# Block products for gate and up (seven of 256 columns for eight), and the down projection as a last stage

## The chip, the cores and the metric

The kernel runs on 1 core of one Trainium2 chip. The metric is the device time of one execution in microseconds (us), from the profiler's clock of that core. The core has five engines with queues of their own: TensorE (PE; its weight loads are shown apart as PEld), VectorE (DVE), ScalarE (ACT), GpSimd (POOL) and SyncE (SP), which issues all the large DMAs here in the order of its own queue.

## The reference

One encoder layer on 512 tokens, d = 2048, in float32. Attention (a differential and a latent half, not touched here) gives `mix`; then an output projection and a gated feed-forward network of 5632 features. The six vectors of `mod` scale, shift and gate.

```python
mod = c_act @ w_ada[l] + b_ada[l]
sh1, sc1, gt1, sh2, sc2, gt2 = [m[:, None, :] for m in jnp.split(mod, 6, axis=-1)]
...
mix = jnp.concatenate([a_out, b_out], axis=-1) @ w_out[l]
x = x + gt1 * mix
h2 = rms_norm(x, g_norm2[l]) * (1 + sc2) + sh2
ffn = (jax.nn.silu(h2 @ w_gate[l]) * (h2 @ w_up[l])) @ w_down[l]
x = x + gt2 * ffn
```

## The kernel before

**Arithmetic.** Every float32 product is made of three matmuls (`mm3`, lines 231 to 233): both operands are split into a high part (a cast, `hi`, line 79 on ACT) and a low part (the difference, `lo`, line 87, in turn on DVE and on POOL), and high x high, high x low and low x high are summed in PSUM.

**Weights.** The class `Weights` follows a plan, a list of chunks of 128 x 1024 float32 (512 KB) in the order of use. A chunk is loaded by SP (line 62) into one of three `raw` buffers and split into one of two `hi` and two `lo` buffers; `get` returns a chunk, splits the next and loads the one after it.

**Stages.** The input projection and the attention come first (not touched). The output projection ends at about 972 us of the profile: four column blocks b, each a `project` into four PSUM banks (`ps_o`), with the side work of `second_modulation` between its steps: loads of w_ada (line 289) and multiply-adds into `adaacc` on DVE (line 296), which give the scale and shift of the second norm; `MOD_PACE` says how many such steps go to one step of the projection. `residual` (lines 1048, 1049) adds the block to `x1`, which stays in SBUF, and `transposes` brings it into `x1T`. After `second_norm` the activations h2 lie in SBUF as high and low parts, features on the partitions and 512 tokens in the columns.

**Feed-forward.** `gate_up(j)` makes one pair: 256 gate and 256 up features, 16 steps over d, two blocks of 128 features each, all 512 tokens wide: 192 matmuls of 512 columns. The result act = silu(g) * u is split into `ah` and `al` (line 1160). The 22 pairs go in parts of `PARTS` = 4, 4, 4, 4, 3, 3; after each part `down` multiplies its acts by w_down, again in four column blocks, and adds the product times the gate vector `gt2` to x1 in SBUF; in the last part each tile of x1 is stored. The vector `gt2` itself (`gate2`) is computed as side work of the first `gate_up` calls, with loads of w_ada of its own. The order on PE is that of the program; a scheduler orders the other engines.

## Time and profile before

| | us |
|---|---|
| median of 3 runs (lowest, highest) | 2420.62 (2419.66, 2422.67) |
| the profiled execution | 2424.76 |
| its span in the trace | 2422.9 |
| PE busy in it | 2289.0 |
| DVE busy | 1284.9 |
| ACT busy | 789.7 |
| POOL busy | 786.2 |

The span goes from the first to the last instruction in the trace; the time of the execution has 1.9 us around it. The mean granted clock of TensorE is 0.981 of full speed (1 is 2.4 GHz, 0.5 is 1.2 GHz). The feed-forward part takes the span from about 973 us to its end.

### The profile page before, as it was taken

Reading aid. Unit: us, or ns where it says so; the run is one execution under the profiler, and the core shown is the slowest. Engines: PE = TensorE matmul, PEld = TensorE weight load, DVE = VectorE, ACT = ScalarE, POOL = GpSimd, SP = SyncE. Lnnn points to the kernel's source line nnn. Section 1 sums busy time; section 2 is a strip of 40 time slices with the busy share of each in tenths; the row PEclk is TensorE's granted clock in tenths of the full one; section 3 lists DMA queues with packets and bytes.
Section 4 is the critical chain, followed back from the end, with each engine's and each line's share of the span. In section 5 each row is a group of like instructions: output and inputs, shape, how many; then the busy total and the mean of one; then the engine's idle time right before and its main releaser. Section 6 shows DMA issues by size and latency. Waiting matters only on the chain.

```text
span 2422.9 us, 28819 instructions
## 1 busy us (share of the span) xinstructions
PE 2289.0 (94%) x10998; PEld 1949.5 (80%) x10998; DVE 1284.9 (53%) x1883; ACT 789.7 (33%) x1359; POOL 786.2 (32%) x671
## 2 busy tenths in 40 slices
PE   3878998998999988999999999999999999999999
PEld 2777998997777767788888888888888888888887
DVE  6998876877988479754242114322241224314324
ACT  4433454557555323422212222122212221222121
POOL 1668744436544513121212222221212122222211
PEclk9989999999999989999999999999999999999999
DMA  8765443532433577444232333333233333333333
GB/s 278 211 198 161 137 146 110 178 90 92 151 124 113 182 239 243 152 160 144 89 103 94 97 96 96 96 96 100 93 103 93 99 96 96 96 96 96 95 100 127
DMA packets 262573, 313.11 MB, mean 129 GB/s; under 512 B 13949, under 2 KB 186470, under 8 KB 262306
## 3 DMA queue, kind: packets, MB, share of 16 engines
q1 hardware_dynamic: 261944, 310.91, 40.8%
q8 instruction: 86, 1.41, 0.2%
q10 hardware_dynamic: 490, 0.36, 0.1%
q14 instruction: 53, 0.43, 0.1%
HBM read 306.99 MB, written 4.24 MB: 128 GB/s over the span
## 4 chain that ended last, share of the span: by engine, by line
PE 62%; DVE 3%; DMA 3%; issue 1%; POOL 0%; ACT 0%; SPq 0%; DVEq 0%; POOLq 0%
PE ps_g L231 7%; PE ps_g L233 7%; PE ps_g L232 7%; PE ps_d L232 7%; PE ps_d L231 7%; PE ps_d L233 7%; PE ps_u L233 7%; PE ps_u L232 7%; PE ps_u L231 7%; DMA araw<-in_w_ada_dram 2%; DVE adaacc L296 2%; DVE lo L87 0%; PE ps_o L233 0%; DVE tm L1048 0%; DVE x L1049 0%
## 5 line engine op out<-in xcount | busy, mean ns | idle before, releaser
L87 POOL TENSOR_TENSOR lo<-raw,hi 128x1024 fp32r<-128x1024 f32 (+1 forms) x188 | 439.9, 2340 | 1318.0 <-ACT hi L79 1313.3
L79 ACT CAST hi<-raw 128x1024 fp32r<-128x1024 f32 (+2 forms) x388 | 390.0, 1005 | 1137.9 <-PE ps_d L232 327.9
L87 DVE TENSOR_TENSOR lo<-raw,hi 128x1024 fp32r<-128x1024 f32 (+2 forms) x200 | 234.1, 1171 | 855.1 <-ACT hi L79 854.0
L296 DVE SCALAR_TENSOR_TENSOR adaacc<-araw,c_col,adaacc 128x256 f32<-128x256 f32 (+1 forms) x334 | 296.9, 895 | 34.1 <-DMA araw<-in_w_ada_dram 21.2
L231 PE MATMUL ps_g<-h2h,hi 128*128 128x512 f32 x704 | 274.8, 390 | 1.6 <-ACT h2h L1113 1.6
L233 PE MATMUL ps_g<-h2l,hi 128*128 128x512 f32 x704 | 274.7, 390 | 0.0
L232 PE MATMUL ps_g<-h2h,lo 128*128 128x512 f32 x704 | 274.7, 390 | 0.0
L233 PE MATMUL ps_u<-h2l,hi 128*128 128x512 f32 x704 | 273.9, 389 | 0.0
L231 PE MATMUL ps_u<-h2h,hi 128*128 128x512 f32 x704 | 273.9, 389 | 0.0
L232 PE MATMUL ps_u<-h2h,lo 128*128 128x512 f32 x704 | 273.9, 389 | 0.0
L231 PE MATMUL ps_in<-hi,hh 128*128 128x384 f32 (+2 forms) x704 | 242.6, 345 | 26.5 <-DVE raw_s L480 7.0
L233 PE MATMUL ps_in<-lo,hh 128*128 128x384 f32 (+2 forms) x704 | 235.5, 335 | 8.5 <-POOL lo L87 8.5
L232 PE MATMUL ps_in<-hi,hl 128*128 128x384 f32 (+2 forms) x704 | 234.9, 334 | 1.0 <-POOL hl L370 0.9
L232 PE MATMUL ps_d<-hi,al 128*128 128x512 f32 x512 | 199.5, 390 | 0.0
L231 PE MATMUL ps_d<-hi,ah 128*128 128x512 f32 x512 | 199.4, 389 | 0.0
L233 PE MATMUL ps_d<-lo,ah 128*128 128x512 f32 x512 | 199.2, 389 | 0.0
L231 PEld LDWEIGHTS ps_in<-hi,hh 128*128 128x128 f32 x704 | 138.8, 197 | 33.8 <-issue 9.5
L231 PEld LDWEIGHTS ps_g<-h2h,hi 128*128 128x128 f32 x704 | 132.7, 188 | 29.5 <-ACT h2h L1113 1.9
L233 PEld LDWEIGHTS ps_g<-h2l,hi 128*128 128x128 f32 x704 | 132.5, 188 | 28.3 <-DVE h2l L1114 0.7
L232 PEld LDWEIGHTS ps_g<-h2h,lo 128*128 128x128 f32 x704 | 132.6, 188 | 27.6
L233 PEld LDWEIGHTS ps_u<-h2l,hi 128*128 128x128 f32 x704 | 132.2, 188 | 27.4
L232 PEld LDWEIGHTS ps_u<-h2h,lo 128*128 128x128 f32 x704 | 132.1, 188 | 27.5
(267 smaller groups left out, 3852.9 us busy)
## 6 DMA issues: line engine op xcount, KB each, us to landing
araw<-in_w_ada_dram SPq DMA_DIRECT2D x128, 512.0 KB
raw<-in_w_gate_dram SPq DMA_DIRECT2D x88, 512.0 KB
raw<-in_w_up_dram SPq DMA_DIRECT2D x88, 512.0 KB
raw<-in_w_down_dram SPq DMA_DIRECT2D x88, 512.0 KB
ada<-in_w_ada_dram SPq DMA_DIRECT2D x128, 256.0 KB
raw<-in_w_in_dram SPq DMA_DIRECT2D x128, 192.0 KB
raw<-in_w_out_dram SPq DMA_DIRECT2D x32, 512.0 KB
xs<-in_x_dram SPq DMA_DIRECT2D x16, 256.0 KB
```

The costliest lines, as they stand in the source:

```text
L79: nc.scalar.copy(out=hi[:, :n], in_=raw[:, :n])
L87: e.tensor_tensor(out=lo[:, :n], in0=raw[:, :n], in1=hi[:, :n].bitcast(F32), op=ALU.subtract)
L231: pe.matmul(o, ah, bh, start=start, stop=False)
L232: pe.matmul(o, al, bh, start=False, stop=False)
L233: pe.matmul(o, ah, bl, start=False, stop=stop)
L296: dve.scalar_tensor_tensor(out=acc[:, :width], in0=raw[:, i, :width], scalar=c_col[:, q:q + 1], in1=acc[:, :width], op0=ALU.mult, op1=ALU.add)
```

## The change

Two pairs stay as they were (`STRAIGHT`). For the other 20, gate and up are made as separate **units** of 256 features. A unit's product is cut in two along features, along d and along tokens, and the eight block products are made from seven (the scheme of Strassen in Winograd's form): seven products of a sum of weight blocks (B11, B21, B22 and T1 to T4; 1024 x 128) with a sum of activation blocks (1024 x 256 tokens), 24 matmuls of 256 columns each, the high and low parts as before. The sums of activations (`comb`, seven of them, split) are built once, during the straight pairs (`combine`, run by `between`). The sums of weights are built for each unit on DVE; all splits of a unit's low parts are on DVE too (`prepare`), and the products are put together in a tile `cu` by ACT copies and DVE adds from PSUM (`unit`). Weights come in halves of 1 MB (`load_half`, three buffers `wr`), `hi` and `lo` have three buffers, and `AHEAD` = 2 products are prepared ahead. act goes to DRAM (`actd`), 0.5 MB a pair.

The down projection is one last stage in parts of 2, 4, 4, 4, 4, 4 pairs; `load_acts` reads act back and splits it. Sums over parts are kept in 16 SBUF tiles; x1 is stored to DRAM (`x1d`) in the output projection and read again in the last part but one. `gate2` is side work of parts 1 to 3 of the down stage. In the output projection the loads of w_ada are of 256 KB in place of 512, into 24 slots that x1, x1T and the accumulators share. What runs before the output projection keeps its order on each engine.

```diff
-PARTS = (4, 4, 4, 4, 3, 3)
+PARTS = (2, 4, 4, 4, 4, 4)
+STRAIGHT = 2
+X_SLOTS = 24
+W_BUFS = 3
+AHEAD = 2
+
+PRODUCTS = (("B11", 0, "X"), ("B21", 2, "Z"), ("T2", 5, "X"), ("T1", 4, "W"), ("T3", 1, "X"), ("T4", 3, "Y"),
+            ("B22", 6, "W"))
...
-    def pair(j):
+    for j in range(STRAIGHT):
         for k4 in range(4):
             for n in ("gate", "up"):
                 plan.append(((n, j, k4), [4, 256], rows(a["w_" + n][0], k4 * 512, 4, j * 256, 256), "alt"))
...
+    return plan
+
+
+def down_plan(a):
+    plan, j = [], 0
+    for n in PARTS:
         for b in range(4):
             for q in range(n):
-                plan.append((("down", b, j + q), [2, 512], rows(a["w_down"][0], (j + q) * 256, 2, b * 512, 512),
-                             "alt"))
+                src = a["w_down"][0][(j + q) * 256:(j + q + 1) * 256, b * 512:(b + 1) * 512]
+                plan.append((("down", b, j + q), [2, 512], src.rearrange("(k p) n -> p k n", p=P), "alt"))
         j += n
...
-    mod2 = second_modulation(raws2, accs2, MOD_EARLY, KC, 2)
+    def accs2(dt=F32):
+        return xtile("adaacc", dt)
+
+    mod2 = second_modulation(xtile, accs2, MOD_EARLY, KC, 1)
...
+            sp.dma_start(out=x1d[t * P:(t + 1) * P, b * 512:(b + 1) * 512], in_=x1[t][b])
...
+    def combine(p):
+        a11, a21 = [x1T[p][:, i * 256:(i + 1) * 256] for i in range(2)]
+        a12, a22 = [x1T[p + 8][:, i * 256:(i + 1) * 256] for i in range(2)]
+        r = [xtile("sr") for _ in range(2)]
+        s1, s2, s4 = r[0][:, :256], r[0][:, 256:], r[1][:, :256]
+        dve.scalar_tensor_tensor(out=s1, in0=a21, scalar=shs[:, p:p + 1], in1=a22, op0=ALU.add, op1=ALU.add)
+        dve.scalar_tensor_tensor(out=s2, in0=s1, scalar=SH2[:, p:p + 1], in1=a11, op0=ALU.subtract, op1=ALU.subtract)
+        dve.scalar_tensor_tensor(out=s4, in0=a12, scalar=SH2[:, p + 8:p + 9], in1=s2, op0=ALU.add, op1=ALU.subtract)
+        dve.tensor_tensor(out=s3[:, p], in0=a11, in1=a21, op=ALU.subtract)
+        for i, src in ((4, half_rows(r[0])), (6, s4.unsqueeze(1))):
+            n = src.shape[1]
+            act.copy(out=comb[p][:, i:i + n, 0, :], in_=src)
+            dve.tensor_tensor(out=comb[p][:, i:i + n, 1, :], in0=src, in1=f(comb[p][:, i:i + n, 0, :]),
+                              op=ALU.subtract)
...
+    def load_half(u, kh):
+        if u >= N_UNITS:
+            return
+        j, n = divmod(u, 2)
+        j += STRAIGHT
+        src = a["w_gate" if n == 0 else "w_up"][0][kh * 1024:(kh + 1) * 1024, j * 256:(j + 1) * 256]
+        t = fw[0][1].tile([P, 8, 256], F32, tag="wr", bufs=3, name="wr")
+        sp.dma_start(out=t, in_=src.rearrange("(k p) n -> p k n", p=P))
+        for n in range(2):
+            units.setdefault(u, {})[f"B{kh + 1}{n + 1}"] = t[:, :, tsl(n)]
...
+    def prepare(q):
+
+        if q >= LAST_Q:
+            Wd.split(q - LAST_Q)
+            return
+        u, i = divmod(q, 7)
+        w = units[u]
+        if i == 0:
+            w["T1"], w["T2"] = [wp.tile([P, 1024], F32, tag="lo", bufs=2, name="wt").rearrange(
+                "p (k n) -> p k n", k=8) for _ in range(2)]
+            w["T3"], w["T4"] = w["B12"], w["T2"]
+        out, x, y = {0: ("T1", "B12", "B11"), 1: ("T2", "B22", "T1"), 2: ("T3", "B22", "B12"),
+                     3: ("T4", "B21", "T2")}.get(i, (None,) * 3)
+        src = w[PRODUCTS[i][0]]
+        hi, lo = [fw[0][1].tile([P, 8, P], F32R, tag=n, bufs=W_BUFS, name=n) for n in ("wh", "wl")]
+        act.copy(out=hi, in_=src)
+        if i < 2:
+            minus(w[out], w[x], w[y])
+        minus(lo, src, f(hi))
+        if i in (2, 3):
+            minus(w[out], w[x], w[y])
+        split[q] = hi, lo
+
+    def multiply(q, ps):
+        u, i = divmod(q, 7)
+        _, ci, bk = PRODUCTS[i]
+        wh, wl = split.pop(q)
+        first = bk not in ps
+        if first:
+            ps[bk] = bank(tags[u % 2], "ps_" + bk)[:, :256]
+        for k in range(8):
+            c = comb[k][:, ci]
+            pe.matmul(ps[bk], wh[:, k], c[:, 0], start=first and k == 0, stop=False, skip_group_check=True)
+            pe.matmul(ps[bk], wh[:, k], c[:, 1], start=False, stop=False, skip_group_check=True)
+            pe.matmul(ps[bk], wl[:, k], c[:, 0], start=False, stop=k == 7, skip_group_check=True)
+        return ps[bk]
+
+    def unit(u):
+
+        ps = {}
+        cu = wp.tile([P, 1024], F32, tag="hi", bufs=2, name="cu").rearrange("p (c s) -> p c s", c=4)
+
+        def plus(i, j, b):
+            dve.tensor_tensor(out=cu[:, i], in0=cu[:, j], in1=b, op=ALU.add)
+
+        for i in range(7):
+            q = 7 * u + i
+            if i == 0:
+                load_half(u + 1, 0)
+            prepare(q + AHEAD)
+            b = multiply(q, ps)
+            if i == 0:
+                act.copy(out=cu[:, 0], in_=b)
+            elif i == 1:
+                plus(0, 0, b)
+            elif i == 2:
+                act.copy(out=cu[:, 2], in_=b)
+            elif i == 4:
+                act.copy(out=cu[:, 1], in_=b)
+                plus(3, 1, ps["W"])
+                load_half(u + 1, 1)
+            elif i == 5:
+                plus(1, 1, b)
+            elif i == 6:
+                plus(2, 2, b)
+            if u == N_UNITS - 1 and i in LATE:
+                LATE[i]()
+        return cu
...
+    def load_acts(i):
+        j0 = sum(PARTS[:i])
         r = []
...
+        for kt in range(2 * j0, 2 * (j0 + PARTS[i])):
+            if i == 0:
+                both = wp.tile([P, 1024], F32R, tag=("raw", "lo")[kt % 2], bufs=(3, 2)[kt % 2], name="act0")
+                ah, al = both[:, :512], both[:, 512:]
+                if kt % 4 == 0:
+                    avs = fw[0][1].tile([P, 8, 256], F32, tag="wr", bufs=3, name="av0").rearrange(
+                        "p (k a) b -> p k (a b)", k=4)
+                av = avs[:, kt % 4]
             else:
-                ah, al = slot("ah"), slot("al")
-            act.copy(out=ah, in_=sg)
-            dve.tensor_tensor(out=al, in0=sg, in1=f(ah), op=ALU.subtract)
+                ah, al = [fd[1].tile([P, S], F32R, tag="ax", bufs=32, name="ax") for _ in range(2)]
+                av = fd[1].tile([P, S], F32, tag="x1r", bufs=4, name="av")
+            sp.dma_start(out=av, in_=actd[kt])
+            act.copy(out=ah, in_=av)
+            minus(al, av, f(ah))
             r.append((ah, al))
...
+    def between():
+        for p in range(8):
+            if p == 0:
+                shift_sums()
+            combine(p)
+            if p in (1, 3, 4, 5, 6):
+                yield
+        close_pool(fp)
+        fw.append(open_pool("fw"))
+        load_half(0, 0)
+        load_half(0, 1)
+        yield
+        prepare(0)
+        yield
+        for q in range(1, AHEAD):
+            prepare(q)
...
+    for u in range(N_UNITS):
+        res = unit(u)
+        if u % 2 == 0:
+            g = res
+            act.activation(g, g, AF.Silu)
+        else:
+            ao = wp.tile([P, 1024], F32, tag="raw", bufs=3, name="ao").rearrange("p (c s) -> p c s", c=4)
+            dve.tensor_tensor(out=ao, in0=g, in1=res, op=ALU.mult)
+            j = u // 2 + STRAIGHT
+            sp.dma_start(out=actd[2 * j:2 * j + 2].rearrange("f p s -> p f s"),
+                         in_=ao.rearrange("p (f c) s -> p f (c s)", f=2))
+    turn[0] = 1 if tags[(N_UNITS - 1) % 2] == "tmp" else 0
+    close_pool(hp)
...
+    for i, n in enumerate(PARTS):
         for b in range(4):
             tag = next_tag()
+            spare[0] = "tmp" if tag == "acc" else "acc"
             pss = [bank(tag, "ps_d") for _ in range(NT)]
-            for _ in project(pss, acts, 512, [("down", b, j0 + q) for q in range(len(acts) // 2)]):
+            cs = slice(b * 512, (b + 1) * 512)
+            if b == 1 and 0 < i and i + 1 < n_parts:
+                load_acts(i + 1)
+            if i == n_parts - 2:
+                xr = []
+                for t in range(NT):
+                    xr.append(fd[1].tile([P, S], F32, tag="x1r", bufs=4, name="x1r"))
+                    sp.dma_start(out=xr[t], in_=x1d[t * P:(t + 1) * P, cs])
+            for _ in project(pss, acts[i], 512, [("down", b, j + q) for q in range(n)]):
+                if 0 < i < n_parts - 2:
+                    next(side, None)
+            for t in range(NT):
+                s = sums[t][b]
+                if i == 0:
+                    act.copy(out=s, in_=pss[t])
+                elif i < n_parts - 1:
+                    dve.tensor_tensor(out=s, in0=s, in1=pss[t], op=ALU.add)
+                    if i == n_parts - 2:
+                        dve.tensor_tensor(out=s, in0=s, in1=gt2[:, cs], op=ALU.mult)
+                        dve.tensor_tensor(out=s, in0=s, in1=xr[t], op=ALU.add)
+                else:
+                    tm = fd[1].tile([P, S], F32, tag="x1r", bufs=4, name="tm")
+                    dve.tensor_tensor(out=tm, in0=pss[t], in1=gt2[:, cs], op=ALU.mult)
+                    dve.tensor_tensor(out=s, in0=s, in1=tm, op=ALU.add)
+                    sp.dma_start(out=out[0, t * P:(t + 1) * P, cs], in_=s)
+        if i == n_parts - 3:
+            for _ in side:
                 pass
-            for t in range(NT):
-                residual(pss, b, t, gt2)
-                if last:
-                    sp.dma_start(out=out[0, t * P:(t + 1) * P, b * 512:(b + 1) * 512], in_=x1[t][b])
```

Three places where the order of instructions moves. **DVE, between two gate/up results.** Before, one pair: `lo` is the low part of a chunk, `sg` the Silu'd gate (times up from `ps_u`), `ax` its split; in brackets is what a row waits for (DMAHW a load, and engines by name).

```order
L87 TENSOR_TENSOR lo<-raw,hi 128x1024 [waits DMAHW0_49,Activation_49]
L1154 TENSOR_TENSOR sg<-sg,ps_u 128x512 [waits PE_49]
L1154 TENSOR_TENSOR sg<-sg,ps_u 128x512 [waits PE_49,Activation_49]
L1160 TENSOR_TENSOR ax<-sg,ax 128x512 [waits Activation_49] x2
L87 TENSOR_TENSOR lo<-raw,hi 128x1024 [waits DMAHW2_49,PE_49,Activation_49]
L87 TENSOR_TENSOR lo<-raw,hi 128x1024 [waits DMAHW4_49,PE_49,Activation_49]
```

After, one unit in the middle of the blocks (`wr` is a raw weight half or a sum written over it, `wt` a sum of weight blocks, `wl` a low part, `cu` the unit's result, `ps_Z`, `ps_W` and `ps_Y` products):

```order
L1205 TENSOR_TENSOR wt<-wr 128x1024 [waits DMAHW4_49,DVE_49]
L1250 TENSOR_TENSOR cu<-cu,ps_Z 128x256 [waits PE_49,Activation_49]
L1205 TENSOR_TENSOR wl<-wr,wh 128x1024 [waits Activation_49]
L1205 TENSOR_TENSOR wl<-wt,wh 128x1024 [waits PE_49,Activation_49]
L1205 TENSOR_TENSOR wl<-wr,wh 128x1024 [waits PE_49,Activation_49]
L1205 TENSOR_TENSOR wt<-wr,wt 128x1024 [waits DMAHW6_49,DVE_49]
L1205 TENSOR_TENSOR wr<-wr 128x8x128
L1250 TENSOR_TENSOR cu<-cu,ps_W 128x256 [waits Activation_49]
L1205 TENSOR_TENSOR wl<-wr,wh 128x1024 [waits PE_49]
L1250 TENSOR_TENSOR cu<-cu,ps_Y 128x256 [waits DVE_49,PE_49]
L1205 TENSOR_TENSOR wl<-wr,wh 128x1024 [waits Activation_49]
L1250 TENSOR_TENSOR cu<-cu,ps_W 128x256 [waits PE_49]
```

The row `wt<-wr,wt` with a DMA among its waits is the first that reads the second half of the next unit's weights; three rows of the present unit's and the next unit's work stand behind it and ahead of the add of `ps_Y`.

**SP, the end of the output projection and the first gate and up loads.** Before:

```order
L62 DMA raw<-in_w_out_dram 128x2x512
L289 DMA araw<-in_w_ada_dram 128x2x512 x2
L62 DMA raw<-in_w_out_dram 128x2x512
L289 DMA araw<-in_w_ada_dram 128x2x512 x2
L62 DMA raw<-in_w_gate_dram 128x4x256
L289 DMA araw<-in_w_ada_dram 128x2x512 x2
L62 DMA raw<-in_w_up_dram 128x4x256
L289 DMA araw<-in_w_ada_dram 128x2x512 x4
L62 DMA raw<-in_w_gate_dram 128x4x256
```

After (`x_` with a number is a slot of x1 or of a w_ada load):

```order
L301 DMA x_9961<-in_w_ada_dram 128x512
L1104 DMA x1d<-x_9134 128x512
L301 DMA x_9964<-in_w_ada_dram 128x512
L1104 DMA x1d<-x_9138 128x512
L301 DMA x_9979<-in_w_ada_dram 128x512
L1104 DMA x1d<-x_9142 128x512
L1104 DMA x1d<-x_9146 128x512
L74 DMA raw<-in_w_gate_dram 128x4x256
L74 DMA raw<-in_w_up_dram 128x4x256
L74 DMA raw<-in_w_gate_dram 128x4x256
L74 DMA raw<-in_w_up_dram 128x4x256
L1104 DMA x1d<-x_9135 128x512
```

The w_ada loads that stood between the first gate and up chunks are gone from there, and stores of x1 stand ahead of and behind them.

**SP, where gate 2's w_ada loads stand.** Before, between the weights of the first pairs:

```order
L62 DMA raw<-in_w_gate_dram 128x4x256
L62 DMA raw<-in_w_up_dram 128x4x256
L289 DMA araw<-in_w_ada_dram 128x2x512
L62 DMA raw<-in_w_gate_dram 128x4x256
L289 DMA araw<-in_w_ada_dram 128x2x512 x2
L62 DMA raw<-in_w_up_dram 128x4x256
L289 DMA araw<-in_w_ada_dram 128x2x512 x3
```

After, between the weights of the down stage, at the densest place:

```order
L74 DMA raw<-in_w_down_dram 128x2x512
L301 DMA araw<-in_w_ada_dram 128x2x512 x2
L74 DMA raw<-in_w_down_dram 128x2x512
L301 DMA araw<-in_w_ada_dram 128x2x512 x3
L74 DMA raw<-in_w_down_dram 128x2x512
L301 DMA araw<-in_w_ada_dram 128x2x512 x2
L74 DMA raw<-in_w_down_dram 128x2x512
L297 DMA adaacc<-in_b_ada_dram 1x512
```

They moved from the gate and up chunks to the down chunks, with up to three of them between two chunks.

## Rows read from the trace of the kernel before

**Rows 1.** The page, part 1: busy us, share of the span, instructions.

```profile
PE 2289.0 (94%) x10998; PEld 1949.5 (80%) x10998; DVE 1284.9 (53%) x1883; ACT 789.7 (33%) x1359; POOL 786.2 (32%) x671
```

**Rows 2.** The page, part 4: shares of the chain that ended last.

```profile
PE 62%; DVE 3%; DMA 3%; issue 1%; POOL 0%; ACT 0%; SPq 0%; DVEq 0%; POOLq 0%
```

**Rows 3.** Windows (us): length, busy us (count) by engine, clock, DMA share, GB/s.

```profile
815.00:850.00 35.00, 33.86 (x148) 27.34 (x147) 16.20 (x15) 8.70 (x13) 30.64 (x19) 1.00 0.84 277
850.00:890.00 40.00, 30.47 (x138) 24.86 (x139) 31.50 (x34) 8.89 (x12) 9.30 (x4) 0.94 0.72 238
890.00:930.00 40.00, 40.00 (x169) 33.37 (x169) 31.65 (x43) 10.11 (x17) 5.94 (x3) 0.85 0.77 261
...
950.00:975.00 25.00, 15.89 (x61) 11.67 (x60) 21.39 (x32) 9.70 (x19) 8.21 (x10) 0.70 0.62 205
...
1000.00:1200.00 200.00, 200.00 (x883) 165.28 (x882) 95.15 (x87) 51.51 (x60) 46.25 (x21) 1.00 0.45 145
...
1500.00:2000.00 500.00, 500.00 (x2201) 412.96 (x2200) 140.10 (x133) 113.92 (x124) 109.97 (x46) 1.00 0.31 96
```

**Rows 4.** Timeline of PE in the input projection: start, us, instruction.

```profile
453.89 0.28 PE L232 MATMUL ps_in<-hi,hl 128*128 128x256 f32 x1
...
456.89 0.28 PE L233 MATMUL ps_in<-lo,hh 128*128 128x256 f32 x1
...
476.30 0.33 PE L231 MATMUL ps_in<-hi,hh 128*128 128x256 f32 x1
476.47 0.28 PE L232 MATMUL ps_in<-hi,hl 128*128 128x256 f32 x1
...
480.54 0.28 PE L233 MATMUL ps_in<-lo,hh 128*128 128x256 f32 x1
```

**Rows 5.** The page, part 5, a group of weight loads: busy us, mean ns.

```profile
L231 PEld LDWEIGHTS ps_g<-h2h,hi 128*128 128x128 f32 x704 | 132.7, 188 | 29.5 <-ACT h2h L1113 1.9
```

**Rows 6.** Groups by line and form on DVE, ACT, POOL: busy us, mean ns, idle before.

```profile
L87 DVE TENSOR_TENSOR lo<-raw,hi 128x1024 fp32r<-128x1024 f32 x157 | 192.8, 1228 | 845.0 <-ACT hi L79 844.7 <-DMA raw<-in_w_gate_dram 0.3
L296 DVE SCALAR_TENSOR_TENSOR adaacc<-araw,c_col,adaacc 128x512 f32<-128x512 f32 x154 | 164.0, 1065 | 22.8 <-DMA araw<-in_w_ada_dram 13.8 <-DMA adaacc<-in_b_ada_dram 5.7
...
L1048 DVE TENSOR_TENSOR tm<-ps_d,gt 128x512 f32<-128x512 f32 x96 | 65.7, 685 | 28.4 <-PE ps_d L233 27.8
...
L785 DVE COPY kn<-ps_in 128x256 f32<-128x256 f32 x16 | 6.6, 411 | 0.2 <-issue 0.2
...
L79 ACT CAST hi<-raw 128x1024 fp32r<-128x1024 f32 x308 | 324.1, 1052 | 1084.6 <-PE ps_d L232 327.9 <-PE ps_u L233 279.7 <-PE ps_g L233 207.7
...
L1153 ACT ACTIVATE sg<-ps_g 128x512 f32<-128x512 f32 x44 | 26.2, 595 | 79.3 <-PE ps_g L233 79.3
...
L819 ACT COPY vr<-ps_in 128x256 f32<-128x256 f32 x16 | 6.0, 376 | 0.0
...
L87 POOL TENSOR_TENSOR lo<-raw,hi 128x1024 fp32r<-128x1024 f32 x151 | 367.6, 2435 | 1275.4 <-ACT hi L79 1275.4
```

**Rows 7.** Timeline of DVE and POOL in a down block.

```profile
1216.76 0.69 DVE L1049 TENSOR_TENSOR x<-x,tm 128x512 f32<-128x512 f32 x1
...
1218.08 2.76 DVE L1049 TENSOR_TENSOR x<-x,tm 128x512 f32<-128x512 f32 x1
...
1217.90 2.40 POOL L87 TENSOR_TENSOR lo<-raw,hi 128x1024 fp32r<-128x1024 f32 x1 [8.20 <-ACT hi L79]
```

**Rows 8.** The chain that ended last, 930 to 1010 us: start, us, what.

```profile
945.63 5.63 DMA araw<-in_w_ada_dram
...
953.38 4.30 DMA raw<-in_w_gate_dram
...
958.93 3.49 DMA raw<-in_w_up_dram
```

**Rows 9.** PE's waits from 800 us on: us in total, times, longest.

```profile
PE ps_o L233 <- DVE lo L87: 8.3, 3, 6.6
PE ps_xT L1055 <- DVE x L1049: 7.0, 4, 3.2
```

More of the change, by code (lines that the diff above doesn't have):

```diff
@@ L1099, in hybrid_layer, with h2, half_rows @@
     transposes(3, spare[0])
[L1100 removed]
+    rB = bank(tag, "ps_r")
     for t in range(NT):
[L1102 to L1104 removed]
+        pe.matmul(rB[:, tsl(t)], rstd2[:, t:t + 1].broadcast_to([P, P]), ident, start=True, stop=True)
+    close_pool(fo)
+    close_pool(big_pool)
+    hp, sx = open_pool("hp", "right"), open_pool("sx", "right")
+    comb = [hp[1].tile([P, 7, 2, 256], F32R, tag="comb", bufs=8, name="comb") for _ in range(8)]
+    s3 = sx[1].tile([P, 8, 256], F32, name="s3")
+    def h2(kc, part):
+        i = kc // 8 * 2
+        return comb[kc % 8][:, i:i + 2, part, :]
+    def half_rows(ap):
+        return ap.rearrange("p (a b) -> p a b", a=2)
     def second_norm(k0):
@@ L1162, in gate_up @@
-        return r
-    def down(j0, acts, last):
+                next(between, None)
+        sg = wp.tile([P, 1024], F32, tag="raw", bufs=3, name="sg").rearrange("p (m s) -> p m s", m=2)
+        for m in range(2):
+            act.activation(sg[:, m], pg[m], AF.Silu)
+            dve.tensor_tensor(out=sg[:, m], in0=sg[:, m], in1=pu[m], op=ALU.mult)
+        sp.dma_start(out=actd[2 * j:2 * j + 2].rearrange("f p s -> p f s"), in_=sg)
+    N_UNITS = 2 * (DFF // 256 - STRAIGHT)
+    LAST_Q = 7 * N_UNITS
@@ new lines, in hybrid_layer @@
+    units, split = {}, {}
+    fw = []
+    def load_half(u, kh):
[8 more added lines that the diff above has]
+            units.setdefault(u, {})[f"B{kh + 1}{n + 1}"] = t[:, :, tsl(n)]
@@ new lines, in hybrid_layer @@
+    second_norm(0)
+    def between():
[14 more added lines that the diff above has]
+            prepare(q)
+        yield
+    gate_up(0, iter(()))
+    for j in range(1, STRAIGHT):
+        mid = between() if j == STRAIGHT - 1 else iter(())
+        gate_up(j, mid)
@@ new lines, in hybrid_layer @@
+    for _ in mid:
+        pass
+    tags = ("acc", "tmp") if turn[0] else ("tmp", "acc")
+    for p in range(8):
+        act.copy(out=comb[p][:, 1, 0, :], in_=s3[:, p])
+        minus(comb[p][:, 1, 1, :], s3[:, p], f(comb[p][:, 1, 0, :]))
+    close_pool(sx)
+    LATE = {4: lambda: load_acts(0)}
+    for u in range(N_UNITS):
[9 more added lines that the diff above has]
+                         in_=ao.rearrange("p (f c) s -> p f (c s)", f=2))
@@ new lines, in hybrid_layer, with gate2, raws, accs @@
+    turn[0] = 1 if tags[(N_UNITS - 1) % 2] == "tmp" else 0
+    close_pool(hp)
+    fd = open_pool("fd", "right")
+    sums = [[fd[1].tile([P, 512], F32, tag="sums", bufs=16, name="sums") for _ in range(4)] for _ in range(NT)]
+    gt2 = fd[1].tile([P, D], F32, name="gt2")
+    def gate2():
+        def raws():
+            return wp.tile([P, 1024], F32, tag="raw", bufs=3, name="araw")
+        turns = iter(("hi", "lo", "lo") * 4)
+        def accs(dt=F32):
+            t = next(turns)
+            return wp.tile([P, 1024], dt, tag=t, bufs=2, name="adaacc")
+        def emit(ps, c0, width):
+            dve.tensor_copy(out=gt2[:, c0:c0 + width], in_=ps)
+        for c0 in range(0, D, 512):
+            yield from ada_row(raws, accs, 5, c0, 512, 2, None, emit)
```

123 lines of the change are left out of this document (53 added, 70 removed).

## The prediction

> **What bounds the kernel now.** The busy times first: TensorE (PE) is busy 94% of the span and no other engine over 53% [rows 1]. The chain that ended last agrees: 62% of it is PE work [rows 2]. Next the table by stretches [rows 3]: from 1000 us on PE is busy in every microsecond, at the full clock (2.4 GHz), while DMA takes 0.31 of its time. So in the feed-forward part only PE's own time counts: 2201 matmuls of 512 columns in 500 us, 227.2 ns each. The out projection before it is different: between 815 and 975 us DMA is 0.62 to 0.84 busy, PE is idle in part, and the clock falls, to a mean of 0.70 in its last stretch. There loads and VectorE (DVE) set the pace.
>
> **The change part by part.**
>
> *Fewer, narrower matmuls.* A pair (256 gate and 256 up features) takes 16 x 2 x 2 x 3 = 192 matmuls of 512 columns. Twenty pairs lose them: 3840 x 227.2 ns = 872.4 us. In place come 40 units (one pair's gate or up) of 7 products, each 8 x 3 = 24 matmuls of 256 columns: 6720. The price of one is in the trace, since the input projection has the same shape and type: starts from 453.89 to 456.89 us with 24 others between, 3.00 / 25 = 120 ns, and from 476.47 to 480.54 with 33 between, 4.07 / 34 = 119.7 ns [rows 4]. So 6720 x 120 ns = 806.4 us: **-66 us**. The saving is not an eighth (109 us), since a half-width matmul costs 53% of a wide one. Bounds: 119.7 ns (804 us, -68); and, if each product began with a step like the one at 476.30, 0.17 us in place of 0.12, (23 x 0.12 + 0.17) / 24 = 122 ns (820 us, -52).
>
> Each of these matmuls still brings its own 128x128 weights, and their load takes 188 ns as recorded [rows 5], more than the 120 ns between starts. The row decides that loads overlap: 120 ns is with a load each. The break-even price is 872.4 / 6720 = 129.8 ns. The Trainium skill (TensorE: Matmul & The Clock Gate, Back-to-back issue gap) says that in a stream of load and matmul pairs both set the spacing, with about 81 ns at 128 columns and 131 at 512; drawn straight between them I estimate 98 ns at 256, three quarters of the wide price, by which seven eighths of the work in half-width matmuls would lose: 6720 x 0.75 x 227.2 = 1145 us, 273 more than before. The trace differs on both widths (227 and 120), and the ratio that counts is 0.53.
>
> *VectorE in a unit.* It now does seven splits and four weight sums of 128x1024, 1.228 us each [rows 6]; four adds of 128x256 from PSUM, about 0.41 (a copy of that shape from PSUM [rows 6]); half of a product of 128x1024, 0.6: 13.5 + 1.6 + 0.6 = 15.7 us. ScalarE (ACT): seven casts at 1.052, three copies at 0.376, half a Silu [rows 6]: about 9.5. A unit takes PE 168 x 0.120 = 20.2 us. Both fit, DVE with 4.4 us to spare. GpSimd (POOL) no longer splits: its split took 2.435 us and stretched a DVE add beside it from 0.69 to 2.76 [rows 6, 7], so DVE's uncontended durations are the right ones. This costs 0 while the products hide it.
>
> *The second weight half.* Here the cover is thinnest. Half h1 of unit u+1 (1 MB) needs the third raw buffer, which frees when DVE has split T3: product 1 ends at 5.8 us, a cast and a split follow, about 8.3 us into unit u. In DVE's order the sums T2 and T3 of the next unit (the second waits on that DMA) stand ahead of the add of ps_W and of the remaining splits; the split of B11, for the next unit's first product, must be done at 20.2, with four DVE steps after the landing: about 16.1. So h1 has 7.7 us. Its price is not in the trace. From below: 1.05 MB at the steady stretch's 96 GB/s over its share of 0.31, 310 GB/s: 3.4 us. From above: twice the chain's 4.30 us for a 512 KB load in busy queues, 8.6 us [rows 3, 8]. With queues as quiet as here (2 MB of weights and 0.25 MB of act in 20.2 us, 117 GB/s) I take 5 to 6, near the lower row: hidden, 0. Each microsecond beyond 7.7 would cost 40 us in all; at 8.6, +36.
>
> *Out projection.* Gate 2's vector moves out: about 20 DVE multiply-adds and 5 MB of loads leave this stage. They hold the end of it: the chain from 945 us is gate-2 loads (5.63 us), first weights queued behind them (4.30, 3.49), and multiply-adds between the residuals [rows 8]. PE waits there (8.3 us on splits, 7.0 on the residual x, [rows 9]) and works at a mean clock of 0.70. I give back 8 us. Against it, 4 MB of x1 stores go into the same SP queue, in stretches where DMA is 0.72 to 0.77 busy [rows 3], and loads of the modulation share 24 slots with x1 and its transposes: +3. Net **-5**, from -15 (all these waits) to +8 (the 4 MB at 261 / 0.77 = 339 GB/s is 12 us, if none of it hides, less a part of the gain).
>
> *Seams and the last stage.* Eight rounds of combinations lie under the straight pairs (PE has 43.6 us in each); eight casts and splits of s3 and the first two weights stand at the first seam: +2. At the second, the first two act pairs come back from DRAM, split under the last unit: +2. The down stage keeps its 2112 matmuls (480 us). But gate 2's 32 loads of 512 KB now stand in SP's order among its weights, at the densest 2.3 to one weight load over some 14 loads. A weight load feeds 24 matmuls, 5.45 us; 3.3 x 0.524 MB in that time is 318 GB/s, against the 310 above and 261 / 0.77 = 339 in the out stage [rows 3]. DVE has 4.6 multiply-adds of 1.065 us there (the mean beside POOL's splits) and half a split, 5.5 us [rows 6], just as full. By 310 GB/s 14 steps lose 14 x 0.13 = 2 us; I take +5, from 0 to +15 (14 steps a fifth longer each). The end is the same chain of four residuals: 0.
>
> Sum: -66 - 5 + 4 + 5 = **-62 us**. The profiled execution took 2424.8 us (span 2422.9 and 1.9 around it), 4.1 above the median of 2420.6; so its span would be about 2361, and the median **2358**.
>
> **The rivals.**
> 1. *The unit stalls on h1 or DVE's order* (slower). For: one DMA on which eleven DVE steps depend, a queue of waits in a fixed order. Against: quiet queues. Gains of 62 are used up at 62 / 40 = 1.55 us of stall in a unit, that is a landing about 9.3 us after issue, beyond my upper row. With 2 us: 2358 + 80 = 2438. A stall of half a microsecond: 2378.
> 2. *Narrow matmuls pay for their weights* (slower). If each of the 6720 had to wait for its own 188 ns load: 1263 us, time 2749. The 120 ns of the rows speak against it; the rule of the Trainium skill above points this way, if less far.
> 3. *More is gained*: the out stage's waits all go (-15 in place of -5), and the seams and gate 2 cost nothing: -62 - 10 - 9, about 2339. For: those waits are mostly loads and DVE steps that leave. Against: the stores that come.
> 4. *The down stage waits for gate 2.* If DMA and DVE together make its 14 steps 1.5 to 2.5 us longer, it is 21 to 35 us more than nothing, 16 to 30 more than I count: 2374 to 2388. For: both are full there by the sum above. Against: PE needs only the weights, which are loaded ahead.
> 5. *The change saves no PE time at all because DVE bounds the unit.* It would need 21.8 us a unit (872.4 / 40), 6 above my sum; its splits would have to cost 1.8 us as when POOL contends, and POOL is idle there: about 2420.
>
> **How the numbers follow.** My forecast, with its parts off by some microseconds, 0.5 (2345 to 2372); the larger gain 0.1; the half-microsecond stall or the down stage 0.24; rival 5 0.04; rival 1 in full 0.1; rival 2 0.02. Cutting off the lowest of the gains and the slow cases leaves 2325 to 2405. A measurement tells about 0.2% (4.8 us). Faster 0.85, same 0.03 (most of rival 5), slower 0.12.
>
> **What would show it.** Blocks: 6720 matmuls of 256 columns starting 120 ns apart, PE busy in each stretch at the full clock, from about 1060 to 1866 us. If a unit takes more than 20.2 us, the waits of PE by line say whether wl (DVE) is late, and those of DVE whether the wr load is. The DVE sum per unit should be 15.7 us. In the out stage the idle piece before the first ps_g should be shorter than 3 us and the low clock gone. In the down stage PE should have no gaps, though DMA share comes near 1 for some 75 us. The prediction is wrong if units pass 21.5 us, or if 256-column matmuls in this stream start over 125 ns apart.

## The result, and the profile after

The changed kernel takes 2362.73 us (median of 4 runs, 2359.97 to 2369.43) against 2420.14 (4 runs, 2419.10 to 2422.67): a ratio of 0.9765, 95% interval 0.9741 to 0.979. The forecast was 2358, in a range of 2325 to 2405. The profiled execution has a span of 2363.4 us, 59.5 less than that of before. The sum was near, but two of its terms were not: the block products gained 20 us more than forecast, and the other stages gave back 23 us more.

The page of the changed kernel, part 1 (busy us, share of the span) and the head of part 4 (the chain that ended last):

```profile
PE 2215.7 (94%) x13878; PEld 2012.5 (85%) x13878; DVE 1680.8 (71%) x2376; ACT 965.6 (41%) x1619; POOL 591.3 (25%) x591
...
PE 56%; DVE 5%; DMA 4%; issue 1%; ACT 0%; POOL 0%; SPq 0%; DVEq 0%; ACTq 0%; POOLq 0%
```

Against [rows 1, 2]: PE is still busy 94% of a shorter span, DVE went from 53 to 71%. Next the windows of the changed kernel, one for each stage of its feed-forward part (length, then busy us and count on PE, PEld, DVE, ACT and POOL, clock, DMA share, GB/s): the two straight pairs, the blocks, the down stage.

```profile
973.28:1068.21 94.93, 91.73 (x384) 74.10 (x385) 63.94 (x100) 39.83 (x60) 19.10 (x7) 0.96 0.32 100
1068.21:1854.34 786.13, 785.21 (x6722) 784.48 (x6720) 602.23 (x621) 348.59 (x424) 1.68 (x1) 1.00 0.36 121
1854.34:2358.70 504.36, 496.27 (x2122) 397.62 (x2120) 241.85 (x283) 123.00 (x146) 106.98 (x48) 1.00 0.47 159
```

In the kernel before, the first gate matmul starts at 972.75, the third pair at 1062.69, and the last down matmul starts at 2417.92 and ends at 2418.31. Twenty pairs at 43.6 us are 872.4, so its down work has 2418.3 - 1062.7 - 872.4 = 483.2 us. Stage by stage:

| | before | after | difference | forecast |
|---|---|---|---|---|
| up to the first gate matmul | 972.75 | 973.28 | +0.5 | -5 |
| two straight pairs, first seam | 89.9 | 94.9 | +5.0 | +2 |
| 20 pairs | 872.4 | 786.1 | -86.3 | -66 |
| second seam and down | 483.2 | 504.4 | +21.2 | +7 |
| end | 4.6 | 4.7 | 0 | 0 |

Each column is one execution. Stages that an edit leaves alone differ by some us between the kernels below: the first gate matmul starts at 969.2 to 973.3 us in the eight that keep the changed kernel's output projection, and the 20 pairs take 785.3 to 791.4 us in the nine that keep its blocks. Why they differ stays open.

In the blocks PE has 6720 matmuls in 786.13 us, 117.0 ns each, not 120, with no gap over 0.9 us. DVE took 602.23 / 40 = 15.1 us a unit (forecast 15.7), ACT 8.7. Three groups of DVE's steps between 1100 and 1850 us, by line and form:

```profile
L1205 DVE TENSOR_TENSOR wl<-wr,wh 128x1024 fp32r<-128x1024 f32 x153 | 187.0, 1222 | 68.2 <-ACT wh L1222 68.1
...
L1205 DVE TENSOR_TENSOR wt<-wr,wt 128x1024 f32<-128x1024 f32 x76 | 92.8, 1222 | 4.9 <-DMA wr<-in_w_up_dram 1.9 <-DMA wr<-in_w_gate_dram 1.7
...
L1250 DVE TENSOR_TENSOR cu<-cu,ps_W 128x256 f32<-128x256 f32 x76 | 31.6, 416 | 22.2 <-PE ps_W L1241 22.2
```

The prices read in [rows 6] held (1.228 and 0.41 us). The second weight half, the thinnest cover, is mostly in time: in the timelines of SP and DVE it is issued at 1254.29 and the sum T2 reads it at 1259.72, 5.4 us later, with no wait.

```profile
1254.29 0.37 SPq L1200 DMA_DIRECT2D wr<-in_w_gate_dram  x1
...
1259.72 1.22 DVE L1205 TENSOR_TENSOR wt<-wr,wt 128x1024 f32<-128x1024 f32 x1
```

Now the waits of PE from 800 us on (total us, times, longest), which answer to [rows 9]:

```profile
PE ps_ada L327 <- DVE adaacc L308: 12.1, 2, 10.9
PE ps_d L243 <- DVE lo L98: 8.0, 4, 3.4
PE ps_xT L1064 <- DVE x L1058: 3.4, 2, 2.9
PE ps_o L243 <- POOL lo L98: 3.1, 1, 3.1
PE ps_o L243 <- DVE lo L98: 3.0, 2, 2.5
```

The waits for splits and for the residual fell from 8.3 and 7.0 to 3.0 and 3.4 us, but one of 10.9 us is new: the small ps_ada matmuls wait for the last multiply-add of the modulation. The timeline of PE shows it, ahead of 72 matmuls of the last column block:

```profile
929.86 0.95 PE L327 MATMUL ps_ada<-ones,adaacc 128*128 128x1 f32 x8
941.75 1.44 PE L327 MATMUL ps_ada<-ones,adaacc 128*128 128x1 f32 x6 [10.94 <-DVE adaacc L308]
```

In the windows of the output projection DMA is fuller than in [rows 3] from 850 to 930, and the low clock has moved with the wait, from the end of the stage to its last column block:

```profile
850.00:890.00 40.00, 36.30 (x160) 29.65 (x161) 29.32 (x35) 9.70 (x14) 7.30 (x4) 0.96 0.84 276
890.00:930.00 40.00, 38.28 (x179) 31.67 (x178) 32.00 (x43) 11.91 (x21) 8.06 (x4) 0.96 0.83 278
930.00:950.00 20.00, 9.06 (x44) 7.87 (x43) 12.03 (x18) 2.87 (x7) 1.94 (x1) 0.66 0.52 167
950.00:975.00 25.00, 19.54 (x91) 15.83 (x90) 11.99 (x18) 11.93 (x22) 8.78 (x10) 0.93 0.32 106
```

In the down stage two things cost time. Most of its blocks of 96 matmuls take 22.4 us, that is 233.3 ns a matmul, where the mean of before was 483.2 / 2112 = 228.8. And the three blocks between 1921 and 2000 us take 24.8, 26.9 and 26.5. The chain of that stretch:

```profile
1936.15 5.31 DMA araw<-in_w_ada_dram
1941.55 0.76 DVE adaacc L308
1942.34 2.78 DVE adaacc L308
1945.14 0.76 DVE adaacc L308
1946.10 0.50 issue
1946.60 1.22 DVE lo L98
...
1949.29 5.25 DMA araw<-in_w_ada_dram
```

A weight split (lo) stands behind multiply-adds that wait for gate 2's loads, of 5.3 to 6.4 us each, and this repeats every 13 us. The loads have three buffers, and SP waits for a multiply-add to free one (26 times in the stage, 44.9 us in all).

### The profile page after: what moved, and what is told of

It reads as the page before. It is cut to its first block, busy times and chain, and to the rows that moved or that the text cites. A ratio compares the mean times of both kernels' runs of the same rounds, so it can differ in the third digit from the quotient of the medians.

```text
span 2363.4 us, 35665 instructions
## 1 busy us (share of the span) xinstructions
PE 2215.7 (94%) x13878; PEld 2012.5 (85%) x13878; DVE 1680.8 (71%) x2376; ACT 965.6 (41%) x1619; POOL 591.3 (25%) x591
## 4 chain that ended last, share of the span: by engine, by line
PE 56%; DVE 5%; DMA 4%; issue 1%; ACT 0%; POOL 0%; SPq 0%; DVEq 0%; ACTq 0%; POOLq 0%
PE ps_d L243 6%; PE ps_d L242 6%; PE ps_d L241 6%; PE ps_X L1240 5%; PE ps_X L1239 5%; PE ps_X L1241 5%; PE ps_W L1239 3%; PE ps_W L1240 3%; PE ps_W L1241 3%; DVE adaacc L308 2%; DMA araw<-in_w_ada_dram 2%; PE ps_Z L1240 2%; PE ps_Y L1239 2%; PE ps_Y L1240 2%; PE ps_Z L1239 2%; PE ps_Z L1241 2%
## 5 line engine op out<-in xcount | busy, mean ns | idle before, releaser
L98 POOL TENSOR_TENSOR lo<-raw,hi 128x1024 fp32r<-128x1024 f32 (+1 forms) x108 | 249.2, 2308 | 1429.9 <-ACT hi L90 1406.4
L90 ACT CAST hi<-raw 128x1024 fp32r<-128x1024 f32 (+2 forms) x228 | 220.9, 969 | 455.0 <-PE ps_d L242 276.8
L1240 PE MATMUL ps_X<-comb,wh 128*128 128x256 f32 x960 | 267.7, 279 | 0.0
L1241 PE MATMUL ps_X<-comb,wl 128*128 128x256 f32 x960 | 267.7, 279 | 0.0
L1239 PE MATMUL ps_X<-comb,wh 128*128 128x256 f32 x960 | 267.7, 279 | 0.0
L243 PE MATMUL ps_d<-lo,ax 128*128 128x512 f32 x640 | 253.6, 396 | 8.0 <-DVE lo L98 8.0
L242 PE MATMUL ps_d<-hi,ax 128*128 128x512 f32 x640 | 253.1, 396 | 0.0
L241 PE MATMUL ps_d<-hi,ax 128*128 128x512 f32 x640 | 253.1, 395 | 0.0
L1205 DVE TENSOR_TENSOR wl<-wr,wh 128x1024 fp32r<-128x1024 f32 x160 | 195.5, 1222 | 77.4 <-ACT wh L1222 77.3
L1240 PEld LDWEIGHTS ps_X<-comb,wh 128*128 128x128 f32 x960 | 180.5, 188 | 0.0
L1239 PEld LDWEIGHTS ps_X<-comb,wh 128*128 128x128 f32 x960 | 180.5, 188 | 0.0
L1241 PEld LDWEIGHTS ps_X<-comb,wl 128*128 128x128 f32 x960 | 180.5, 188 | 0.0
L1239 PE MATMUL ps_W<-comb,wh 128*128 128x256 f32 x640 | 179.1, 280 | 0.9 <-DVE cu L1250 0.8
L1240 PE MATMUL ps_W<-comb,wh 128*128 128x256 f32 x640 | 178.5, 279 | 0.0
```

The costliest lines, as they stand in the source:

```text
L90: nc.scalar.copy(out=hi[:, :n], in_=raw[:, :n])
L98: e.tensor_tensor(out=lo[:, :n], in0=raw[:, :n], in1=hi[:, :n].bitcast(F32), op=ALU.subtract)
L241: pe.matmul(o, ah, bh, start=start, stop=False)
L242: pe.matmul(o, al, bh, start=False, stop=False)
L243: pe.matmul(o, ah, bl, start=False, stop=stop)
L1205: dve.tensor_tensor(out=out, in0=x, in1=y, op=ALU.subtract)
```

## Where tiles lie, and what a matmul costs

The down matmuls of before already had two prices: 227 ns where the act operand is an `ah` or `al` tile, 234 ns where it is one of the `ax` tiles (the first pair of a part), alike in shape. Two of their groups in the trace of before (count, busy us, mean ns of one):

```profile
L232 PE MATMUL ps_d<-hi,al 128*128 128x512 f32 x512 | 199.5, 390 | 0.0
...
L232 PE MATMUL ps_d<-hi,ax 128*128 128x512 f32 x192 | 76.1, 396 | 0.0
```

A matmul runs into the next, so the means are longer than the time from start to start; they differ by the same 6 to 7 ns. What differs in the built program is the address. Some tiles begin at a multiple of 64 bytes, some 32 beside one. With the moving operand first and the stationary one second, as remainders of 64 bytes: the input projection, gate and up before are (0, 0), the `ax` part of down (0, 32); after, the input projection and the straight pairs are (32, 32), the blocks (32, 0), all of down (0, 32). This gave the theory of the first, fourth, eighth and eleventh runs.

## The experiments

The theory: the gain is that of the block products alone, and what the other stages lose has three causes of its own, the places of the act tiles, the order of gate 2's steps and the place of one ps_ada group. The rival: the gain is small in itself or comes from the stages around it, and these losses are the price of more DMA and VectorE work, wherever it stands. Twelve kernels, in the order in which they ran. Times are medians with the ratio to the kernel before and its interval; three kernels (the third, fourth and eighth) ran once and have one time.

**Act tiles moved by 32 bytes.**

```diff
+    dve.memset(fd[1].tile([P, 8], F32, name="pad"), 0.0)
     close_pool(fd)
```

> The changed kernel with one spare tile of 32 bytes a partition in the pool of the down stage, so that the act tiles (the stationary operand of all down matmuls) begin 32 bytes lower: at a multiple of 64 bytes, as the moving weights do. In the changed kernel and in a third of the down matmuls of the kernel before, act tiles lie 32 bytes off a multiple of 64 and a matmul starts every 234 ns; where both operands lie at a multiple of 64 it is 227. Theory A (the place of the tiles sets it): down matmuls 227 ns apart, 20 of the 22 blocks of 96 matmuls 21.8 us in place of 22.4, down stage 12 us shorter, time about 2350. Theory B (the order of the stage or DMA beside it sets it): 233 ns as before, time about 2362.

2357.59 us (0.9738, 0.9722 to 0.9754). Down matmuls start 227 ns apart, blocks without gate 2 take 21.76 us; windows of this run (884 matmuls in 200 us, where the changed kernel has 859):

```profile
2100.00:2300.00 200.00, 200.00 (x884) 1.00 0.39 129
```

Theory A holds. The stage took 496.5 us in place of 504.4, 8 less and not 12: in the four blocks with gate 2's loads (23.8, 24.9, 26.1 and 28.1 us) the loss over the others grew from 11 to 16 us. Why it grew is not shown.

**Gate 2 at every second step.**

```diff
+    turns2 = [0]
...
-                if 0 < i < n_parts - 2:
+                turns2[0] += 1
+                if 0 < i < n_parts - 2 and turns2[0] % 2:
                     next(side, None)
```

> The changed kernel with one step of gate 2 for every second step of the down projection in place of every step. Theory A (the gate-2 sums with their loads stand ahead of the weight splits on VectorE, and the density does it): the four waits of TensorE between 1935 and 1977 us go, blocks of 24.8, 26.9 and 26.5 us become 22.4, about 11 us less: 2351. Theory B (the loads and the splits share DMA and VectorE whatever the density): the waits spread over more blocks, and the time stays within 3 us of 2362.

2360.17 us (0.975, 0.9734 to 0.9766); the down stage 498.4 us, 6.0 less. This does not decide between the theories, since the edit did not do what it says: the scheduler, which orders SP and DVE, still put up to three gate-2 loads between two weight loads (at 1903, 1917, 1939 and 1968 us). The ninth run repeats it with the order forced.

**Twelve straight pairs, ten in blocks.**

```diff
-STRAIGHT = 2
+STRAIGHT = 12
```

> The changed kernel with 12 straight pairs and 10 in block products, in place of 2 and 20. Theory A (the gain is that of the block products): a straight pair takes 43.6 us and one in block products 39.3, so 10 pairs fewer cost 43 us: about 2405. Theory B (the gain comes from the other parts, or the blocks gain only by what the straight pairs lose): less than 15 us more than 2362.

2405.94 us, 43.2 over the changed kernel. The windows of its 12 straight pairs and of its 10 pairs in blocks:

```profile
970.26:1499.17 528.91, 526.22 (x2304) 433.59 (x2305) 127.05 (x160) 135.36 (x160) 114.61 (x47) 1.00 0.34 108
1499.17:1895.30 396.13, 395.27 (x3361) 394.84 (x3360) 300.24 (x311) 175.32 (x214) 1.67 (x1) 1.00 0.36 120
```

Theory A: the gain is that of the block products, 4.3 us a pair.

**The kernel before in halves.** Both halves open their sums in the same bank, and the results are not those of the layer; number, shape and order of the instructions are as told, and the run is read for its time alone.

```diff
-    mm3(pp[m], wh[:, i, tsl(m)], wl[:, i, tsl(m)], hh, hl, kc == 0, kc == KC - 1)
+    for hs in (slice(0, 256), slice(256, 512)):
+        o, st, sp_ = pp[m][:, hs], kc == 0, kc == KC - 1
+        pe.matmul(o, wh[:, i, tsl(m)], hh[:, hs], start=st, stop=False, skip_group_check=True)
...
```

> The kernel before with each gate and up matmul of 512 columns cut in two of 256, with the same weights loaded for both: 8448 matmuls in place of 4224, no other part changed. Theory A (the price of a 256-column matmul is that of the input projection, 120 ns, whatever it is part of): 4224 x (240 - 227) = 55 us more, about 2475. Theory B (117 ns, as in the blocks): 4224 x 6.6 = 28 us more, 2448. Theory C (narrow matmuls pay for their weight load of 188 ns): 4224 x (376 - 227) = 629 us more, 3050.

2477.35 us, 57 over before. The window of this run:

```profile
1110.00:1200.00 90.00, 90.00 (x749) 1.00 0.30 93
```

A matmul starts every 120 ns: theory A. Weights were loaded twice as often, so B and C fall for this place. By the Trainium skill (TensorE: Matmul & The Clock Gate, Back-to-back issue gap), whose 81 ns at 128 columns and 131 at 512 I had drawn to 98 at 256, this edit would have cost 4224 x (2 x 98 - 131) = 275 us, an estimate; the trace (120 and 227 ns) does not agree with it at either width.

**Down weights split two chunks ahead.**

```diff
+        def get(self, key):
+            i = self.at
+            r = super().get(key)
+            self.split(i + 2)
+            self.load(i + 3)
+            return r
```

> The changed kernel with the weights of the down stage split two chunks ahead in place of one (the three hi and lo buffers allow it). Theory A (in gate 2's blocks a weight split waits on VectorE behind multiply-adds whose loads are late by 5 to 6 us, longer than the one chunk of 5.6 us that TensorE has in hand): with two chunks in hand the waits before 1935, 1948, 1962 and 1977 us go and the down blocks all take about 22.4 us: 11 us less, about 2352. Theory B (DMA or VectorE is short over the whole of these blocks): the same loss, later: within 3 us of 2362.

2364.32 us (0.9768, 0.9752 to 0.9784); the down stage 506.0 us, with four waits of 1.4 to 3.2 us where they were. Theory A as put fell: to ask for a split one chunk earlier saves nothing. The timeline of DVE in this run shows why:

```profile
1940.45 5.23 DVE L308 SCALAR_TENSOR_TENSOR adaacc<-araw,c_col,adaacc 128x512 f32<-128x512 f32 x4 [1.67 <-DMA araw<-in_w_ada_dram]
1945.60 1.22 DVE L98 TENSOR_TENSOR lo<-raw,hi 128x1024 fp32r<-128x1024 f32 x1
```

The split of a later chunk stands in the same queue, behind the same multiply-adds. What two chunks really in hand would be worth is not shown.

**A slower modulation pace in the last column block.**

```diff
-MOD_PACE = (0.3, 2.8, 3.4, 3.2)
+MOD_PACE = (0.3, 2.8, 3.4, 1.0)
```

> The changed kernel with 1.0 modulation steps in place of 3.2 to a step of the last column block of the output projection, which moves the second group of small ps_ada matmuls 28 rows later in TensorE's order. Theory A (the place in the order: matmuls that could run stand behind a wait of 10.9 us for the last multiply-add): the wait falls under 5 us and the first gate matmul starts 5 to 8 us earlier than 973.3: about 2356. Theory B (the loads of the stage bound it, and its end follows the last of them): the wait shrinks, but the residuals and transposes come as late: no more than 2 us.

2356.26 us (0.9727, 0.9712 to 0.9743). The wait fell to 0.6 us:

```profile
939.12 1.05 PE L327 MATMUL ps_ada<-ones,adaacc 128*128 128x1 f32 x8 [0.62 <-DVE adaacc L308]
```

The first gate matmul starts at 962.0 in place of 973.3. The eight kernels without this edit start it at 969.2 to 973.3, the four with it at 960.4 to 964.2, so the edit is worth about 9 us in the stage; the median fell by 6.5. Theory A.

**The straight pairs' splits on VectorE.**

```diff
-                plan.append(((n, j, k4), [4, 256], rows(a["w_" + n][0], k4 * 512, 4, j * 256, 256), "alt"))
+                plan.append(((n, j, k4), [4, 256], rows(a["w_" + n][0], k4 * 512, 4, j * 256, 256), "dve"))
```

> The changed kernel with all weight splits of the two straight pairs on VectorE, none on GpSimd. Theory A (the 5 us that these pairs take more than before come from GpSimd's splits, which stretch the combination steps from 0.4 to 2.5 us and so delay the next split): no combination step over 1 us, the waits before 1021 and 1023 us go, the pairs take 95 us less 3 to 5: about 2359. Theory B (VectorE has too much to do in the second pair): the pairs get longer, 2362 or more.

2361.62 us (0.9747, 0.9727 to 0.9768): in the time no difference to be told, but the trace shows the stage. The pairs took 91.1 us in place of 94.9 (94.2 to 95.8 in the kernels that keep this stage), and the waits before 1021 and 1023 us are gone; the blocks, which the edit leaves alone, took 791.4 us in this run, 5.3 more. A combination step in this run, and in the changed kernel:

```profile
L1152 DVE SCALAR_TENSOR_TENSOR sr<-x1T,SH,sr 128x256 f32<-128x256 f32 x8 | 3.8, 480 | 0.1
```

```profile
L1152 DVE SCALAR_TENSOR_TENSOR sr<-x1T,SH,sr 128x256 f32<-128x256 f32 x8 | 5.9, 740 | 0.0
```

Theory A. The Trainium skill (GPSIMD Engine Reference, Specifications) says that GpSimd shares its SBUF interfaces with VectorE and that instructions with two SBUF inputs collide there; 480 and 740 ns agree.

**Activation sums moved by 32 bytes**, to (0, 0) in the blocks and (0, 32) in the straight pairs.

```diff
     s3 = sx[1].tile([P, 8, 256], F32, name="s3")
+    pad = hp[1].tile([P, 8], F32, name="pad")
```

> The changed kernel with 32 spare bytes in the pool of the activation sums, so that these, the moving operand of the block products and of the straight pairs, begin at a multiple of 64 bytes and no longer 32 beside one; the weights stay where they are. Theory A (what counts is how the places of the two operands stand to each other): block matmuls, now both at a multiple of 64 as in the input projection of the kernel before, take 120 ns in place of 117, 20 us more in all; the matmuls of the straight pairs (moving at a multiple, stationary 32 beside it, as in the down stage) 234 ns in place of 227, 3 us more: about 2385. Theory B (the stationary operand's place alone): 117 ns still, the straight pairs 227 still: 2362.

2386.3 us. Block matmuls 120.0 ns apart, those of the straight pairs 232 to 235: both of theory A's numbers. The window of this run, where the changed kernel has 2574 matmuls:

```profile
1500.00:1800.00 300.00, 299.49 (x2496) 1.00 0.36 120
```

**Gate 2's steps queued behind weight splits and loads.**

```diff
...
+    step = [0]
...
-                if 0 < i < n_parts - 2:
-                    next(side, None)
+                step[0] += 1
+                if 0 < i < n_parts - 2 and step[0] % 2:
+                    with tc.issue_after(Wd.last["lo"]), tc.issue_after(Wd.last["load"]):
+                        next(side, None)
```

> The changed kernel with gate 2's steps, one for every second step of the down projection, queued on VectorE behind the last weight split there and on SP behind the last weight load: one load of w_ada now stands between two loads of weights, in place of up to three. Theory A (density: at up to three loads between two the multiply-adds wait for loads while weight splits stand behind them): no wait of TensorE over 0.5 us in the down stage, blocks of 22.4 us, down stage 493 us in place of 504: about 2352. Theory B (it is the amount of gate-2 work, wherever it stands): the loss is spread over more blocks, the stage takes 500 us or more: 2358 to 2363.

2352.49 us (0.9719, 0.9698 to 0.9739). PE has no wait in the down stage, which takes 494.8 us. The stretch from 1921 to 2000 us, in this run and in the changed kernel:

```profile
1921.00:2000.00 79.00, 79.00 (x341) 63.59 (x340) 42.81 (x53) 20.51 (x24) 17.84 (x9) 1.00 0.57 186
```

```profile
1921.00:2000.00 79.00, 70.92 (x299) 55.43 (x299) 66.96 (x77) 18.51 (x23) 15.79 (x7) 1.00 0.72 241
```

Theory B falls: it is not the amount, since the same 32 loads, at one between two weight loads, cost nothing that shows. For theory A one rival is left. The edit changes two things, the density of the loads and the place of gate 2's steps behind the last weight split and load, and no run has the second without the first.

**Three edits at once**: act tiles, pace, straight splits, as above.

> The changed kernel with three of the edits above at once: act tiles moved by 32 bytes, the slower modulation pace in the last column block, the straight pairs' splits on VectorE. If these act in different stages and add up: down blocks 21.8 us, first gate matmul at about 962 us, straight pairs 91 us: 12 + 10 + 4 us less the waits for gate 2 that grow by some 5 as in the first run: about 2342. If gate 2's stage takes it back: 2350.

2340.8 us (0.9668, 0.9641 to 0.9696): the stages add up. The first gate matmul is 9.1 us earlier, the pairs take 90.4 us (4.5 less), the down stage 494.1 (10.3 less), and the blocks 1.6 more, 22.3 in all. Gate 2's waits remain (blocks of 25.7 and 30.3 us).

**The same with the down weights 32 bytes up**, (32, 0) in all parts of the down stage but the first; the buffers are 1040 numbers wide, the blocks use the first 1024.

```diff
-                t = fw[0][1].tile([P, 8, P], F32R, tag="w" + kind[0], bufs=W_BUFS, name=kind)
+                t = fw[0][1].tile([P, 1040], F32R, tag="w" + kind[0], bufs=W_BUFS, name=kind)
+                return t[:, 8:1032]
...
```

> The same three edits, and the down weights (the moving operand of the down matmuls) 32 bytes up in their buffers, so that they stand to the act tiles as the activation sums stand to the weights in the block products: moving 32 beside a multiple of 64, stationary at one. If that place gives back 3 ns a matmul at 512 columns as it does at 256 (117 against 120): down matmuls 224 ns apart, 20 blocks of 21.5 us: 6 us less than the run with three edits. If the 3 ns belong to 256 columns alone: 227 ns and the same time as that run.

2349.83 us (0.9696, 0.9682 to 0.971). Neither expectation: the matmuls start 233 ns apart, as at (0, 32), 9 us over the run before it. Its first part, whose act tiles lie elsewhere, is now at (32, 32), and 192 matmuls from 1839.95 to 1884.30 us start 231 ns apart, not 227:

```profile
1839.95 0.39 PE L241 MATMUL ps_d<-hi,act 128*128 128x512 f32 x1
...
1884.30 0.39 PE L241 MATMUL ps_d<-hi,ax 128*128 128x512 f32 x1
```

**All four edits.**

> The three edits (act tiles moved by 32 bytes, the slower pace in the last column block, the straight pairs' splits on VectorE) and gate 2's steps queued behind the weight splits and loads. If the down stage's loss in the run with three edits (494 us, where 2112 matmuls at 226.8 ns take 479) is gate 2's waits alone: no wait over 0.5 us there, 480 to 482 us, time 13 us under the 2341 of that run: about 2328. If a down stage with shorter blocks leaves gate 2 too little time even when thinned: blocks of over 22.5 us among those with gate 2's loads, and 2335 or more.

2329.18 us (5 runs, 0.9614, 0.9596 to 0.9633): 33.5 us less than the changed kernel, 90 less than before. Its down stage, straight pairs and blocks, to be read against the windows of the changed kernel:

```profile
1842.60:2324.90 482.30, 482.10 (x2122) 397.74 (x2120) 231.08 (x285) 123.71 (x146) 105.74 (x48) 1.00 0.50 166
960.45:1052.36 91.91, 89.34 (x385) 72.99 (x385) 65.80 (x107) 39.69 (x60) 0.00 (x0) 0.98 0.33 103
1052.36:1842.60 790.24, 790.24 (x6721) 790.14 (x6720) 602.67 (x621) 348.60 (x424) 1.67 (x1) 1.00 0.36 121
```

## Why the prediction was right, and where it was not

1. **The block products: mechanism right, price 3 ns too high.** The -66 us stood on 120 ns from [rows 4]. The rows are right for both operands at a multiple of 64 bytes, and the eighth run gives that price back when the sums are moved there. At (32, 0) it is 117 ns (116.9 to 117.9 as the mean of a run's blocks), so the term is -86. My bounds, 119.7 to 122, came from one place of the tiles only. The third run ties the whole gain to these products.
2. **DVE and the second weight half: right, with less cover than said.** DVE took 15.1 us for 15.7. (ScalarE's terms add to 9.1, not 9.5; it took 8.7.) Rival 1 did not happen: DVE waited 4.1 us in all for the weight halves, in six waits over 40 units. But "h1 has 7.7 us" is too much: DVE comes to the half 5.4 us after its issue, and the one time that it could read it only after 6.9 us, PE waited 0.85 us (at 1164.9).
3. **The output projection: wrong.** "I give back 8 us" failed. Gate 2's work did leave the end of the stage, and the waits for splits and residuals shrank; but a wait of 10.9 us for the modulation took their place, since the second ps_ada group stands in PE's order ahead of work that was ready. The sixth run moved it, and the stage then gave about 9 us. The forecast had looked at which loads leave, not at which row PE meets next. What the x1 stores cost by themselves (forecast +3) no run shows.
4. **The seams: +4 forecast, +5 found**, all at the first. "Eight rounds of combinations lie under the straight pairs" left out that POOL still splits there and stretches them; the seventh run took back 3.8 us.
5. **The down stage: wrong by 14 us, in two steps.** "Keeps its 2112 matmuls (480 us)" failed: they cost 9 to 10 us more (2112 x (233.3 - 228.8)), because all act tiles now lie where before those of 6 pairs in 22 did; the first run shows it. The 11 to 12 us that are left are gate 2's waits, forecast as 5 within 0 to 15: the way of rival 4, at half of its lower price (21 us). "Against: PE needs only the weights, which are loaded ahead" left out that the weights have to be split too. DMA was at 0.71 to 0.80 between 1890 and 1980 us, not near 1; what PE waited for was a split in DVE's queue behind multiply-adds whose loads were late. The fifth run shows the split there, and in the ninth, where the steps stand behind the splits and half as dense, the waits are gone.
6. **Rival 2** (narrow matmuls pay for their loads) has no sign of it: twice the loads in the fourth run left 120 ns, and in the blocks 117. Its time was added up wrongly, too: 1263 us in place of 806 on top of 2358 is 2815, not 2749.

So the right sum came from errors of opposite sign, and a median 5 us off says less for the working than the table of stages does.

## What to carry to other kernels

A price for an instruction that has the same shape elsewhere in the trace is a price for that place: look whether the same form already has two prices in the rows (here 227 and 234 ns for one line), and find what tells them apart, before multiplying one by thousands. When work leaves a stage, follow the queue of the engine that waited to its next row that needs something late, for the wait goes there. A side computation with loads of its own is to be spread by the order that reaches the queues; bunched ahead of the splits it cost 11 us, and the same work behind them, at one load per chunk, nothing.
